# A hybrid mLSTM and DeltaNet block: queries turned from PSUM, mLSTM heads at one step of the units, their outputs written by GpSimd and read further ahead

## The chip, the cores and the metric

One core of a Trainium2 chip runs the whole kernel. The metric is the device time of one execution in microseconds; several runs are made of a kernel and their median is compared. TensorE (PE), VectorE (DVE), ScalarE (ACT), GpSimd (POOL) and SyncE (SP) each work through a queue of their own, in order; DMA transfers are started by SyncE, ScalarE or GpSimd and are carried out beside all of them.

## What is computed

One decoder layer with two branches on 512 tokens of width 2048. The input is normalised and multiplied with one wide matrix w_in; its columns are the inputs of an mLSTM branch (8 heads), of a gated DeltaNet branch (16 heads) and of two merge gates. The part that matters here is the mLSTM head and what becomes of its output:

```python
q = q * (dk ** -0.5)
scores = jnp.einsum('cbhtd,cbhsd->cbhts', qc, kc)
...
num = (inter_w[..., None] * jnp.einsum('bhtd,bhde->bhte', q_c, C)
       + jnp.einsum('bhts,bhse->bhte', intra_w, v_c))
...
h_a = _merge_heads(_rmsnorm(h_a)) * ml_norm_w.astype(jnp.float32)
h_a = h_a * jax.nn.sigmoid(ml_o) * jax.nn.silu(ml_z)
...
y_a = jnp.matmul(h_a, w_out[:ML_WIDTH])
y_b = jnp.matmul(h_b, w_out[ML_WIDTH:])
return jax.nn.sigmoid(gate_a) * y_a + jax.nn.sigmoid(gate_b) * y_b
```

The queries carry the factor 1/sqrt(128); it may as well be put on the keys, since queries and keys only meet in products. The sum with the residual is normalised once more at the end.

## The kernel before

All big products are made of three passes: each operand is split into a high part (`split_hi`, L139, a cast on ScalarE: `wh`) and the rest (`split_lo`, L142, a subtraction on VectorE: `wl`), so a block of weights must be loaded by SyncE, cast and subtracted before TensorE can use it. Weights are loaded four tiles and split three tiles ahead.

The program has four stages.

1. The input is normalised, turned and split, and the first four mLSTM heads' queries and keys are projected (`proj_cm`).
2. `seven_stage` makes the other columns that don't need a convolution, in blocks of two times 512 columns with seven products instead of eight (z, s, q, v and g of the list `SEVEN`). Its sums of weights (`ts`, tag `tg`, three buffers in the pool `wp`) are written to DRAM and read back for the second half of a block. At the end of a block a sink takes the finished tiles out of PSUM: `sink_q` (L730) takes queries and keys of heads 4 to 7. The tiles m1 and m5 come first, U1 and C22, which hold sums in SBUF, after them. Each is scaled or copied on ScalarE, transposed in blocks of 32 by 32 on VectorE into a tile `to` of tag `tg` (L738) and written to DRAM by four DMAs on ScalarE's queue (L744), one of them at each tick, in the arrangement that the heads read later (`qt_d`). Keys are also written unturned (`k_d`, L735).
3. The mixers: eight units (`dn_unit`), each with three projections K, V and Q of two DeltaNet heads. `proj_cm` calls `tick()` 16 times, so a unit has 48 ticks; `tick()` lets generators started with `start(gen, wait)` go on, each up to its next `yield n`, which lets n ticks pass. In this way the order of TensorE's queue is written out by hand: small products of the mixers stand between the big ones. In a unit `dn_front_k` (products `pk`, L902, whose input `kq` is finished by `silu_end`, L837, on VectorE), `dn_front_q`, `dn_back` (products p1 to p4) and `dn_chain` follow each other, partly within the next unit. `ml_head(h)` is started at tick 1 + 42 h. 42 and 46 ticks after its start it multiplies its two output tiles by their gates (`mg`, L1228) and calls `turn(g, hm_d, True)`: a transpose on VectorE into a tile `to` (tag `to`, two buffers, which the values' and the DeltaNet outputs' turns use too, L853), and five ticks later four DMAs of 64 KB into `hm_d` from ScalarE's queue (L863). In the last unit `load_h` (L1248) reads the pairs of `hm_d` back, two pairs ahead, into tiles that the heads have used, and splits each (`uh` on ScalarE, L1245, `ul` on VectorE, L1246).
4. The output projection: two wide blocks with the mLSTM half, one with the DeltaNet half, then blocks with seven products again, and `last_block` for the last 512 columns, for which `load_hm` (L1514) reads tiles of `hm_d` once more, two of them by SyncE and the rest by ScalarE after each split.

TensorE's queue has the order of the code. On the other engines a scheduler orders the instructions, by its own estimate of time and by priority: `urgent(n)` raises it, and `behind("A")` puts an instruction after the newest weight split of that engine ("S": after the newest weight load of SyncE).

Of the kernel before, what the change touches and what calls it, by code (L numbers as in the profile page):

```python
# [15 lines left out]
P = 128  # L16
# [30 lines left out]
UNITS = list(range(8))  # L47
QKS = 2 * QKFIRST * P
# [9 lines left out]
def hybrid_body(  # L58
# [671 lines left out]
    def sink_q(c1, c2, m1, m5, m7, last):  # L730

        def turned(x_, c, a):
            if a:
                with behind("A"):
                    nc.scalar.dma_start(k_d[c], x_)  # L735
            o = spare(True)
            with behind("V"):
                V.transpose(o, x_)  # L738
            to = qt_d[a * 4:(a + 1) * 4].rearrange("h (j r) (n a c) -> r (h j) n a c", r=BS, n=NC, c=BS)
            ov = o.rearrange("p (m c) -> p m c", c=BS)  # L740
            for b in range(4):
                yield 1
                with behind("A"):
                    nc.scalar.dma_start(to[:, :, c, b, :], ov[b * BS:(b + 1) * BS])  # L744

        def out_(ps, t, a, wait):
            z = spare(False)
            with urgent(3):
                A.mul(z, ps, (float(P) ** -0.5, 1.0)[a])
            start(turned(z, t, a), wait + 6 * t)  # L750

        def end5(t):
            add(m5[t], U1[t], m5[t])
            out_(m5[t], t, 1, 8)

        def late_q(t):
            with behind("A"):
                A.mul(U1[t], U1[t], float(P) ** -0.5)
            yield from turned(U1[t], 2 + t, 0)

        def end7(t):
            add(U1[t], U1[t], m7[t])
            start(turned(C22[t], 2 + t, 1), 14 + 6 * t)
            start(late_q(t), 17 + 6 * t)

        return (lambda t: out_(m1[t], t, 0, 4)), end5, end7
# [82 lines left out]
    def turn(src, dst, out=False, lag=5):  # L849


        o = dst if dst is not src and len(dst.shape) == 3 else wk.tile([P, NC, P], F32, tag="to", name="to", bufs=2)
        V.transpose(o if len(src.shape) == 3 else o.rearrange("p n c -> p (n c)"), src)  # L853
        start(travel(o, dst, out, lag > 3), lag if out else 2)

    def travel(o, dst, out, apart):
# [3 lines left out]
        if out:  # L860
            for a in range(4):
                with behind("A"):
                    nc.scalar.dma_start(d[:, :, a, :].rearrange("m r c -> r m c"), ov[a * BS:(a + 1) * BS])  # L863
                if apart:
                    yield 1
            return
# [175 lines left out]
    def dn_chain(j, hs, kq, u, soon):  # L1042
# [60 lines left out]
        turn(g, h_d[h], True, 5 if h < 2 * UNITS[-1] else 3)  # L1103
# [34 lines left out]
    def ml_head(h):  # L1138
# [87 lines left out]
        for i in range(2):  # L1226
            with behind("V"):
                V.tensor_tensor(out=g[i], in0=v1[:, :, i * P:(i + 1) * P], in1=g[i], op=ALU.mult)  # L1228
            turn(g[i], hm_d[2 * h + i], True)
# [18 lines left out]
    def load_h():  # L1248
# [3 lines left out]
        def load():  # L1252
            if len(raws_) < KH:
                if len(raws_) % 2:
                    r = wkb.tile([P, NC, NB + 1], F32, tag="mv1", name="hr", bufs=1)
                    r = r.rearrange("p c n -> p (c n)")[:, 0:2 * S].rearrange("p (a s) -> p a s", s=S)
                else:
                    r = wkb.tile([P, 2, S], F32, tag="mkq", name="hr", bufs=1)
                for n in range(2):
                    load_tile(r[:, n, :], hm_d[2 * len(raws_) + n])  # L1260
                raws_.append(r)

        load()
        load()
        yield 4
        for i in range(KH):
            for n in range(2):
                k = 2 * i + n
                split_scaled(uh[:, k, :], ul[:, k, :], raws_[i][:, n, :], normc[:, 16 + k:17 + k])
# [4 lines left out]
    for h in range(MLH):  # L1274
        start(ml_head(h), 1 + 42 * h, "B")
# [238 lines left out]
    def load_hm():  # L1514
# [3 lines left out]
        def load(q):  # L1518
            r = fin["pool"].tile([P, NO], F32, tag="hmr", name="hmr", bufs=3)
# [4 lines left out]
        for _ in range(2):  # L1524
            load(nc.sync)
        yield 4
# [11 lines left out]
    def sink_last(c1, c2, m1, m5, m7):  # L1538
# [3 lines left out]
        def half_b():  # L1542
# [5 lines left out]
            start(load_hm(), 5)  # L1548
# [185 lines left out]
```

## Time and profile before

| | |
|---|---|
| median of 3 runs | 2212.88 us (2210.53 to 2216.82) |
| profiled execution | 2213.26 us, span 2211.5 us |
| granted TensorE clock, mean | 0.993 |
| ACT's writes hm_d<-to | 64 of 64 KB, 4.1 us to landing |
| ACT's writes qt_d<-to | 32 of 64 KB, 4.0 us to landing |
| SP's reads hr<-hm_d | 16 of 256 KB, 4.2 us to landing |
| hmr<-hm_d | 14 by ACT (4.9 us to landing), 2 by SP (5.4 us) |

In the profile's rows a group or a waiting instruction is named by its line, its operation and its tiles ("kq<-th,kq": kq written from th and kq). A number in square brackets is the time for which the engine stood idle before the instruction, with what released it. A wait for several things is put down to the one that came last.

### The profile page before, as it was taken

The page shows a single profiled execution, that of the slowest core. Times are in us where ns is not written, and L with a number is a line of the kernel's source. Part 1 is how long each engine was busy: PE and PEld are TensorE (multiplying, and loading weights), DVE is VectorE, ACT ScalarE, POOL GpSimd, SP SyncE. Part 2 cuts the span into 40 slices and gives each one's busy share as a digit, 9 for nine tenths or more (in the row PEclk, how much of TensorE's full clock was granted, in tenths as well). Part 3 has the DMA queues.
Part 4 walks back from the last instruction along what each step waited for, and adds up shares of the span by engine and source line. Part 5 has one row for each costly group of instructions (what it writes and reads, how often), then busy time and mean ns, then how long its engine had stood idle before and what let it go on. Part 6 is the DMA issues. An engine that isn't in the chain of part 4 may idle for free.

```text
span 2211.5 us, 31646 instructions
## 1 busy us (share of the span) xinstructions
PE 2146.4 (97%) x10544; PEld 1761.4 (80%) x10544; DVE 1698.6 (77%) x2937; ACT 1035.6 (47%) x1996; POOL 291.4 (13%) x395
## 2 busy tenths in 40 slices
PE   6999999999999999999999999999999999999997
PEld 5877777878887888888888888887877887877785
DVE  5787788788878777777857788778778776578886
ACT  5444444444444444444445545545445464344345
POOL 0320000000000000000012422324314121110200
PEclk9999999999999999999999999999999999999998
DMA  5456676667668757776867677768768577687886
GB/s 157 122 180 189 196 215 191 213 195 231 201 217 240 232 186 231 233 223 189 262 203 176 168 186 183 180 153 208 175 160 213 141 189 193 186 261 212 242 281 222
DMA packets 532006, 444.20 MB, mean 201 GB/s; under 512 B 250369, under 2 KB 385762, under 8 KB 531714
## 3 DMA queue, kind: packets, MB, share of 16 engines
q1 hardware_dynamic: 400946, 350.33, 55.2%
q10 hardware_dynamic: 124192, 74.02, 10.9%
q0 software_dynamic: 6704, 17.83, 3.6%
q8 instruction: 82, 1.34, 0.3%
q14 instruction: 82, 0.67, 0.1%
HBM read 348.66 MB, written 97.58 MB: 202 GB/s over the span
## 4 chain that ended last, share of the span: by engine, by line
PE 65%; DMA 14%; DVE 10%; issue 4%; ACT 2%; SPq 2%; POOL 1%; ACTq 0%; DVEq 0%; POOLq 0%
PE ps L577 11%; PE ps L578 11%; PE ps L576 10%; PE pj L256 8%; PE pj L257 8%; PE pj L258 8%; DVE wl L142 4%; DMA wr<-t_d 3%; DMA wr<-in_w_in_dram 2%; ACT wh L139 2%; DMA wr<-in_w_out_dram 1%; SPq L504 1%; DVE t L518 1%; DMA hr<-h_d 1%; PE py L1369 1%
## 5 line engine op out<-in xcount | busy, mean ns | idle before, releaser
L139 ACT CAST wh<-wr 128x512 fp32r<-128x512 f32 (+1 forms) x522 | 373.1, 717 | 388.8 <-PE pj L257 189.9
L142 DVE TENSOR_TENSOR wl<-wr,wh 128x512 fp32r<-128x512 f32 (+1 forms) x522 | 442.3, 850 | 144.1 <-ACT wh L139 137.1
L256 PE MATMUL pj<-uh,wh 128*128 128x512 f32 x896 | 373.6, 417 | 1.8 <-ACT yp L821 1.8
L258 PE MATMUL pj<-uh,wl 128*128 128x512 f32 x896 | 351.3, 392 | 0.0
L257 PE MATMUL pj<-ul,wh 128*128 128x512 f32 x896 | 350.9, 392 | 0.0
L577 PE MATMUL ps<-wl,uh 128*128 128x512 f32 x752 | 296.8, 395 | 5.7 <-DVE wl L142 5.1
L576 PE MATMUL ps<-wh,uh 128*128 128x512 f32 x752 | 294.7, 392 | 2.7 <-DVE X L630 2.4
L578 PE MATMUL ps<-wh,ul 128*128 128x512 f32 x752 | 294.0, 391 | 0.0
L139 ACT CAST wh<-ts 128x512 fp32r<-128x512 f32 x240 | 148.2, 617 | 256.4 <-DVE ts L536 209.6
L139 ACT CAST wh<-t 128x1024 fp32r<-128x1024 f32 x120 | 126.3, 1052 | 270.1 <-PE ps L578 144.1
L577 PE MATMUL ps<-wl,suh 128*128 128x512 f32 x624 | 243.1, 390 | 4.1 <-DVE wl L142 4.1
L576 PE MATMUL ps<-wh,suh 128*128 128x512 f32 x624 | 243.5, 390 | 1.0 <-ACT wh L139 0.5
L578 PE MATMUL ps<-wh,sul 128*128 128x512 f32 x624 | 242.9, 389 | 0.0
L258 PEld LDWEIGHTS pj<-uh,wl 128*128 128x128 f32 x896 | 168.7, 188 | 37.2
L256 PEld LDWEIGHTS pj<-uh,wh 128*128 128x128 f32 x896 | 169.5, 189 | 32.3 <-ACT yp L821 2.3
L257 PEld LDWEIGHTS pj<-ul,wh 128*128 128x128 f32 x896 | 169.6, 189 | 28.2
L142 DVE TENSOR_TENSOR wl<-ts,wh 128x512 fp32r<-128x512 f32 x240 | 164.4, 688 | 35.2 <-ACT wh L139 35.2
L142 DVE TENSOR_TENSOR wl<-t,wh 128x1024 fp32r<-128x1024 f32 x120 | 147.4, 1228 | 52.6 <-ACT wh L139 51.9
L577 PEld LDWEIGHTS ps<-wl,uh 128*128 128x128 f32 x752 | 141.8, 189 | 44.2 <-DVE wl L142 15.7
L576 PEld LDWEIGHTS ps<-wh,uh 128*128 128x128 f32 x752 | 141.7, 188 | 36.1 <-DVE X L630 6.3
L578 PEld LDWEIGHTS ps<-wh,ul 128*128 128x128 f32 x752 | 141.9, 189 | 28.7
L536 DVE TENSOR_TENSOR ts<-wr 128x512 f32<-128x512 f32 x120 | 82.8, 690 | 100.1 <-DMA wr<-t_d 77.8
(319 smaller groups left out, 3587.6 us busy)
## 6 DMA issues: line engine op xcount, KB each, us to landing
wr<-in_w_in_dram SPq DMA_DIRECT2D x744, 256.0 KB, 3.7
wr<-in_w_out_dram SPq DMA_DIRECT2D x138, 256.0 KB, 4.7
t_d<-ts ACTq DMA_DIRECT2D x104, 256.0 KB, 4.0
wr<-t_d SPq DMA_DIRECT2D x104, 256.0 KB, 3.9
xt<-in_x_dram SPq DMA_DIRECT2D x8, 512.0 KB, 7.4
tg_d<-X ACTq DMA_DIRECT2D x16, 256.0 KB, 5.6
tg_d<-to ACTq DMA_DIRECT2D x16, 256.0 KB, 6.0
v<-v_d SPq DMA_DIRECT2D x8, 512.0 KB, 5.2
```

The lines of the kernel that those rows point to most:

```text
L139: newest["A"] = A.copy(hi, src).ins
L142: newest["V"] = V.tensor_tensor(out=lo, in0=src, in1=hi.bitcast(F32), op=ALU.subtract).ins
L256: T.matmul(ps[j], hi[:, k, wsl], uh[:, kt, :], start=(kt == 0), stop=False)
L257: T.matmul(ps[j], hi[:, k, wsl], ul[:, kt, :], start=False, stop=False)
L258: T.matmul(ps[j], lo[:, k, wsl], uh[:, kt, :], start=False, stop=(kt == KT - 1))
L504: newest["S"] = nc.sync.dma_start(to, src).ins
L518: V.tensor_tensor(out=t13, in0=r[:, 1:3, :], in1=r[:, 0:2, :], op=ALU.subtract)
L536: V.tensor_tensor(out=ts[:, 0, :], in0=r[:, 0, :], in1=r[:, 2, :], op=ALU.subtract)
L576: T.matmul(ps[t], ah, hi, start=(g == "A" and i == 0), stop=False, skip_group_check=True)
L577: T.matmul(ps[t], ah, lo, start=False, stop=False, skip_group_check=True)
L578: T.matmul(ps[t], al, hi, start=False, stop=(i == KH - 1), skip_group_check=True)
L1369: T.matmul(ps[c], uh[:, kt, tsl], hi, start=(kt == ks[0]), stop=False)
```

## The change

Five things are changed together.

- `sink_q`: m1 is transposed straight from PSUM, unscaled; the factor 1/sqrt(128) goes onto the keys (m5 when it is copied, C22 later). The turned tiles come from tag `wr` (`spare(False)`, four buffers of the pool `wp`) and not `tg`. Their four DMAs are issued by GpSimd, two at a tick. k_d is still written by ScalarE.
- `HEADS`: the heads start at 1, 41, 85, 130, 178, 226, 274 and 322 instead of 1 + 42 h; from head 3 on the step is 48, a unit's ticks.
- `turn(..., out)` takes an engine: the mLSTM outputs are written to hm_d by GpSimd, DeltaNet's h_d by ScalarE as before.
- `load_h` keeps three pairs in flight, and puts its splits behind the weights'.
- `load_hm` reads four tiles ahead, behind the weight loads, into two tags in turn, and starts two ticks earlier.

```diff
+HEADS = (1, 41, 85, 130, 178, 226, 274, 322)
...
     def sink_q(c1, c2, m1, m5, m7, last):
 
-        def turned(x_, c, a):
+        def place(o, c, a):
+            to = qt_d[a * 4:(a + 1) * 4].rearrange("h (j r) (n a c) -> r (h j) n a c", r=BS, n=NC, c=BS)
+            ov = o.rearrange("p (m c) -> p m c", c=BS)
+            for b in range(4):
+                G.dma_start(to[:, :, c, b, :], ov[b * BS:(b + 1) * BS])
+                if b % 2:
+                    yield 1
+
+        def turned(x_, c, a, scale):
+            if scale:
+                with behind("A"):
+                    A.mul(x_, x_, float(P) ** -0.5)
             if a:
                 with behind("A"):
                     nc.scalar.dma_start(k_d[c], x_)
-            o = spare(True)
+            o = spare(False)
             with behind("V"):
                 V.transpose(o, x_)
...
-            for b in range(4):
-                yield 1
-                with behind("A"):
-                    nc.scalar.dma_start(to[:, :, c, b, :], ov[b * BS:(b + 1) * BS])
-
-        def out_(ps, t, a, wait):
+            yield 1
+            yield from place(o, c, a)
+
+        def end1(t):
+            o = spare(False)
+            with urgent(3):
+                V.transpose(o, m1[t])
+            start(place(o, t, 0), 2 + 3 * t)
+
+        def end5(t):
+            add(m5[t], U1[t], m5[t])
             z = spare(False)
             with urgent(3):
-                A.mul(z, ps, (float(P) ** -0.5, 1.0)[a])
-            start(turned(z, t, a), wait + 6 * t)
...
+                A.mul(z, m5[t], float(P) ** -0.5)
+            start(turned(z, t, 1, False), 10 + 4 * t)
 
         def end7(t):
             add(U1[t], U1[t], m7[t])
-            start(turned(C22[t], 2 + t, 1), 14 + 6 * t)
-            start(late_q(t), 17 + 6 * t)
+            start(turned(U1[t], 2 + t, 0, False), 16 + 3 * t)
+            start(turned(C22[t], 2 + t, 1, True), 22 + 4 * t)
...
-                with behind("A"):
-                    nc.scalar.dma_start(d[:, :, a, :].rearrange("m r c -> r m c"), ov[a * BS:(a + 1) * BS])
+                with behind("A") if out is nc.scalar else ExitStack():
+                    out.dma_start(d[:, :, a, :].rearrange("m r c -> r m c"), ov[a * BS:(a + 1) * BS])
...
-            turn(g[i], hm_d[2 * h + i], True)
+            turn(g[i], hm_d[2 * h + i], G)
...
-                if len(raws_) % 2:
+                m = len(raws_) % 3
+                if m == 2:
                     r = wkb.tile([P, NC, NB + 1], F32, tag="mv1", name="hr", bufs=1)
...
+                elif m:
+                    r = [wkb.tile([P, NC, P], F32, tag=t, name="hr", bufs=1).rearrange("p c n -> p (c n)") for t in ("mkw", "mw")]
...
-        load()
-        load()
-        yield 4
+        for _ in range(3):
+            load()
+            yield 1
+        yield 1
         for i in range(KH):
             for n in range(2):
                 k = 2 * i + n
-                split_scaled(uh[:, k, :], ul[:, k, :], raws_[i][:, n, :], normc[:, 16 + k:17 + k])
+                with behind("A"), behind("V"):
+                    split_scaled(uh[:, k, :], ul[:, k, :], raws_[i][n], normc[:, 16 + k:17 + k])
...
     for h in range(MLH):
-        start(ml_head(h), 1 + 42 * h, "B")
+        start(ml_head(h), HEADS[h], "B")
...
-            r = fin["pool"].tile([P, NO], F32, tag="hmr", name="hmr", bufs=3)
+            if len(raws_) % 2:
+                r = late["sb"].tile([P, NO], F32, tag="hs", name="hmr", bufs=4)
+            else:
+                r = fin["pool"].tile([P, NO], F32, tag="hmr", name="hmr", bufs=3)
...
-        for _ in range(2):
-            load(nc.sync)
-        yield 4
+        for _ in range(4):
+            with behind("S"):
+                load(nc.sync)
+            yield 1
...
-            start(load_hm(), 5)
+            start(load_hm(), 3)
```

Line numbers of the changed kernel lie one to seventeen above those of before (its `wl` is L143, its casts `wh` L140). What the scheduler makes of it is shown at three places.

ScalarE while the block of queries is turned, before (`wh` are the weight casts, `t` and `ts` the weight sums, `to` the turned tiles):

```order
L744 DMA qt_d<-to 32x16x32 x5
L139 CAST wh<-t_5931 128x1024
L744 DMA qt_d<-to 32x16x32
L139 CAST wh<-ts 128x512
L532 DMA t_d<-ts 128x512
L139 CAST wh<-wr_5843 128x512
L744 DMA qt_d<-to 32x16x32 x2
L735 DMA k_d<-to 128x512
L139 CAST wh<-t_5983 128x1024
```

And in the changed kernel, at the same weight sums:

```order
L140 CAST wh<-t_5928 128x1024
L747 DMA k_d<-to 128x512
L140 CAST wh<-ts 128x512
L533 DMA t_d<-ts 128x512
L140 CAST wh<-wr_5845 128x512
L140 CAST wh<-t_5980 128x1024
L140 CAST wh<-ts 128x512
```

The writes of turned tiles are gone from ScalarE's queue; on GpSimd's they stand as one run of 32. The weight casts, the write of the sums (t_d) and k_d stay.

VectorE in unit 5 about the first product of `dn_front_k`, before (`mg` is a head's output, `kq` the keys that `pk` needs, `aq` made from `pk`, `ke` the turned keys, `tn` a turned solution of the small systems):

```order
L1228 TENSOR_TENSOR mg<-v_14522,mg 128x512
L830 SCALAR_TENSOR_TENSOR kq_14846<-yp_9799,convc,kq_14846 128x512
L837 SCALAR_TENSOR_TENSOR kq_14845<-th,kq_14845 128x512
L853 STREAM_TRANSPOSE to<-mg 128x512
L142 TENSOR_TENSOR wl<-wr,wh 128x512
L964 STREAM_TRANSPOSE tn<-tt 128x256
L830 SCALAR_TENSOR_TENSOR kq_14846<-yp_9799,convc,kq_14846 128x512
L853 STREAM_TRANSPOSE ke<-kq_14845 128x512
L1228 TENSOR_TENSOR mg<-v_14522,mg 128x512
L142 TENSOR_TENSOR wl<-wr,wh 128x512
L985 TENSOR_SCALAR qe<-qe 128x8
L853 STREAM_TRANSPOSE to<-mg 128x512
```

In the changed kernel, in the same unit:

```order
L843 SCALAR_TENSOR_TENSOR kq_14815<-th,kq_14815 128x512
L859 STREAM_TRANSPOSE ke<-kq_14815 128x512
L910 TENSOR_TENSOR aq<-pk,dm 128x4x128
L913 SCALAR_TENSOR_TENSOR jd,nk<-aq,ident 128x128 x3
L143 TENSOR_TENSOR wl<-wr,wh 128x512
L1017 TENSOR_TENSOR vt<-vt,nk 128x512 x2
L913 SCALAR_TENSOR_TENSOR jd,nk<-aq,ident 128x128
L910 TENSOR_TENSOR aq<-pk,dm 128x4x128
L143 TENSOR_TENSOR wl<-wr,wh 128x512
L913 SCALAR_TENSOR_TENSOR jd,nk<-aq,ident 128x128
L1234 TENSOR_TENSOR mg<-v_14830,mg 128x512
```

Before, both outputs and their turns stand among the last steps of kq; now the second kq and both aq stand ahead of the first output.

ScalarE in the last unit, where `load_h` splits what it has read (`uh<-hr`), before (`w` are the copies of `dn_chain`):

```order
L1245 ACTIVATE uh<-hr,normc 128x512
L1067 COPY w<-pw 128x128 x2
L139 CAST wh<-wr 128x512
L836 ACTIVATE th<-vt 128x512
L1245 ACTIVATE uh<-hr,normc 128x512 x3
L139 CAST wh<-wr 128x512
L1245 ACTIVATE uh<-hr,normc 128x512 x2
L139 CAST wh<-wr 128x512
L1067 COPY w<-pw 128x128 x2
```

In the changed kernel:

```order
L1251 ACTIVATE uh<-hr,normc 128x512
L1073 COPY w<-pw 128x128 x2
L140 CAST wh<-wr 128x512
L842 ACTIVATE th<-vt 128x512
L1251 ACTIVATE uh<-hr,normc 128x512
L140 CAST wh<-wr 128x512
L1251 ACTIVATE uh<-hr,normc 128x512
L140 CAST wh<-wr 128x512
L1251 ACTIVATE uh<-hr,normc 128x512
L1073 COPY w<-pw 128x128 x2
```

Before, five splits stand between two pairs of copies, three and two of them in a row; now there are three, each behind a weight cast.

19 lines of the change are left out of this document (6 added, 13 removed).

## The prediction

> **What bounds the kernel now.** I read the page's busy times first, then who waits for whom on TensorE, then that view again in short stretches, to place each wait.
>
> ```profile
> span 2211.5 us, 31646 instructions
> PE 2146.4 (97%) x10544; PEld 1761.4 (80%) x10544; DVE 1698.6 (77%) x2937; ACT 1035.6 (47%) x1996; POOL 291.4 (13%) x395
> ```
> ```profile
> PE pprm L107 <- POOL rs L303: 14.8, 1, 14.8
> PE ps L577 <- DVE wl L142: 9.7, 12, 2.4
> PE pk L902 <- DVE kq L837: 8.6, 4, 5.4
> PE ps L576 <- DVE X L630: 2.4, 3, 0.9
> ```
>
> TensorE is busy for 2146.4 of 2211.5 us, and the change takes no matmul away. So a gain can only come out of the 65.1 us (2211.5 - 2146.4) in which it is idle, and 14.8 of those are the start, which the change doesn't touch. The rest are single waits. These stretches hold the ones near the changed places: 699 to 705 us, 1505 to 1520, 1595 to 1612, 1680 to 1704, 1815 to 1840 and 2165 to 2187, in this order (columns: us in total, times, longest).
>
> ```profile
> PE ps L577 <- DVE wl L142: 2.4, 1, 2.4
> PE ps L576 <- ACT wh L139: 0.2, 1, 0.2
> ...
> PE pk L902 <- DVE kq L837: 1.8, 2, 1.5
> ...
> PE pk L902 <- DVE kq L837: 5.4, 1, 5.4
> ...
> PE pj L256 <- ACT yp L821: 1.8, 1, 1.8
> PE pk L902 <- DVE kq L837: 1.4, 1, 1.4
> ...
> PE pw L1064 <- DVE r L1059: 1.4, 1, 1.4
> PE pr L1056 <- DVE st L1077: 1.4, 1, 1.4
> PE pst L1071 <- ACT w L1067: 1.2, 2, 1.0
> ...
> PE py L1369 <- ACT uh L1245: 1.5, 1, 1.5
> PE py L1369 <- ACT wh L139: 1.1, 1, 1.1
> PE py L1371 <- DVE ul L1246: 1.0, 2, 0.7
> PE py L1370 <- DVE wl L142: 0.4, 1, 0.4
> ```
>
> A long wait costs more than itself: the granted clock falls to half behind it. Three stretches at 0.50 (second number after the busy time) follow the waits at 701, 1605 and 2183 us.
>
> ```profile
> 704.75:708.16 3.41, 3.41 (x10) 0.50 0.80 176
> 1609.28:1616.10 6.83, 5.27 (x17) 0.50 1.09 285
> 2186.13:2189.54 3.41, 3.41 (x9) 0.50 0.00 0
> ```
>
> At half the clock, half of the busy time is lost: 1.7, 2.6 and 1.7 us. So the change can reach, at most: A (the block of queries, 699 to 708) 2.4 + 0.2 + 1.7 = 4.3 us; B (units 4 to 6 of the mixers) 1.8 + 5.4 + 1.8 + 1.4 + 2.6 = 13.0; C (the last unit) 4.0; D (the last block) 4.0 + 1.7 = 5.7. Together 27.0 us. I sum against the profiled execution's own time, 2213.3 us (its span and 1.8 us around it), 0.4 above the median of the runs, 2212.9.
>
> **A: the queries turned from PSUM.** Before, 32 writes to qt_d stand in ScalarE's queue, and the turned tiles share three buffers with the weight sums.
>
> ```profile
> L744 ACTq DMA_DIRECT2D qt_d<-to x32: 309/458/1631, 672.7 to 714.1; - x32
> ...
> 685.49 1.05 ACT L139 CAST wh<-t 128x1024 fp32r<-128x1024 f32 x1 [4.54 <-DMA qt_d<-to]
> 697.02 1.05 ACT L139 CAST wh<-t 128x1024 fp32r<-128x1024 f32 x1 [4.09 <-DMA qt_d<-to]
> ...
> 702.29 0.71 DVE L738 STREAM_TRANSPOSE to<-X 128x512 f32<-128x512 f32 x1 [1.10 <-DMA qt_d<-to]
> ```
>
> ScalarE's next weight cast stands 4.54 and 4.09 us behind such writes, VectorE 1.10 us behind a buffer, and the wait of 2.4 us on wl follows. The change takes all 32 out of that queue (its order in the section on the change shows it) and gives the tiles the four buffers of tag wr. So both releasers go. What it adds: two transposes of 0.71 us at the block's end, urgent on VectorE, where it has its sums to do; two scalings on ScalarE go, with no price, since that engine is 47% busy. The nearest wait for such work at a block's end is 2.4 us over three times, 0.9 at most: bounds 0 and 0.9 us, and I take 0.9, because VectorE is nearly full there. A gives -3.4.
>
> GpSimd has nothing else in that stretch. It has to issue 32 writes of 512 runs of 128 B each, which no row shows. Bounds:
>
> ```profile
> L863 ACTq DMA_DIRECT2D hm_d<-to x64: 309/318/1182, 1208.7 to 1770.1; - x64
> DMA to landing us min/median/max: 2.0/4.0/6.2
> ...
> L811 POOL DMA_DIRECT2D gb<-rows_d x16: 536/618/627, 1150.4 to 1768.3; - x16
> DMA to landing us min/median/max: 4.0/5.0/7.2
> ...
> L1565 POOL DMA_DIRECT2D ty<-tg_d x1: 727/727/727, 2109.1 to 2109.1; - x1
> ```
>
> ScalarE issues the same shape in 0.32 us. GpSimd takes 0.62 us for 128 rows and 0.73 for 256 rows, 0.11 us more. If that step holds, 512 rows cost 0.73 + 2 x 0.11 = 0.95 us; if the cost is in proportion to the rows, 4 x 0.62 = 2.5. I take 1.0, by the pair of rows on GpSimd itself, and keep 0.6 and 2.5 as ends. At 1.0, 32 writes fill 32 of the 41 us in which they were issued before; a tile is due again only after four others, so up to some 2 us each VectorE doesn't meet a buffer still held.
>
> The Trainium skill (DMA: Bandwidth & Descriptors, section "Issuing engines are not separate DMA queues") speaks against this: moving the start of a DMA to another engine saves only the sequencer's time for issuing it, usually small. By it A would be worth nothing and the forecast 3.4 us higher. The rows above speak for A: ScalarE is held not by its issues of 0.46 us, but by what those wait for (4.54 us).
>
> **B: the heads at one step of the units.** A projection has 16 ticks, a unit 48. By the code, dn_front_k's first product pk stands at tick 24 and 25 of a unit, and its input kq is finished (L837) from tick 20 and 23. A head's outputs (mg, L1228, and their transposes) come 42 and 46 ticks after its start. Before, with a step of 42, they fall to ticks 43/47, 37/41, 31/35, 25/29, 19/23, 13/17, 7/11 and 1/5 of units 0 to 7. The waits on pk are in units 4, 5 and 6 alone, where they come ahead of pk. In unit 5 VectorE does this:
>
> ```profile
> 1599.40 0.68 DVE L1228 TENSOR_TENSOR mg<-v,mg 128x512 f32<-128x512 f32 x1
> 1600.67 0.68 DVE L837 SCALAR_TENSOR_TENSOR kq<-th,kq 128x512 f32<-128x512 f32 x1
> ...
> 1604.88 0.69 DVE L1228 TENSOR_TENSOR mg<-v,mg 128x512 f32<-128x512 f32 x1
> ...
> 1610.01 0.68 DVE L837 SCALAR_TENSOR_TENSOR kq<-th,kq 128x512 f32<-128x512 f32 x1
> ```
>
> Both outputs precede the second kq, for which TensorE stood 5.4 us. While they fall to ticks 25 to 41 (units 1 to 3), there is no wait at all:
>
> ```profile
> 1150.00:1450.00 300.00, 300.00 (x1747) 250.94 (x1745) 234.05 (x580) 161.93 (x420) 97.82 (x135) 1.00 0.75 181
> ```
>
> TensorE is busy for 300.00 of 300.00 us there. The new starts put heads 1 to 7 at 35/39, 31/35 and five times 28/32, between positions that cost nothing. All of a head's earlier steps move by the same amount, so they too lie between those of heads 2 and 3 before. For heads 4 to 7 VectorE's order has both kq and the first aq ahead of mg. The wait on yp (1.8 us) belongs to head 6's late position as well. What is late next is the previous unit's dn_back, ticks 25 to 33, beside the four moved operations of 0.7 us. Bounds: nothing, or every one of the 13.0 us back; I leave two waits of 1.4 us, the size of the smaller ones here. B gives 2.8 - 13.0 = -10.2.
>
> With 64 writes of hm_d GpSimd gets 64 x 1.0 = 64 us of work within some 620. Its next work there (nk, dm, ke, we, mkq) is due most of a unit later. ScalarE loses 64 x 0.32 = 20 us of issues, and the waits behind them.
>
> **C and D: reading ahead.** Before, splits of the heads' outputs hold ScalarE until their rows land, in the last unit and in the last block:
>
> ```profile
> 1827.49 1.55 ACT L1245 ACTIVATE uh<-hr,normc 128x512 fp32r<-128x512 f32 x2 [3.83 <-DMA hr<-hm_d]
> ...
> 2168.78 0.72 ACT L1245 ACTIVATE uh<-hmr,normc 128x512 fp32r<-128x512 f32 x1 [4.56 <-DMA hmr<-hm_d]
> ```
>
> The copies w and the weight casts queue behind them, and TensorE waits for those. With three pairs in flight instead of two, a read starts 10 ticks ahead of its split, not 6; in the last block four tiles ahead, not two. How long a tick is, the row of pk tells:
>
> ```profile
> L902 PE MATMUL pk<-kq x128: 270/275/552, 1172.9 to 1790.3; 128*128 128x128 f32 x128
> ```
>
> From unit 0's first to unit 7's last are 617.4 us for 7 x 48 + 1 ticks, 1.83 us each. Four ticks are 7.3 us, more than the 3.83 us; splits now also follow the newest weight split. Against it: head 7 starts 27 ticks later (322, not 295), so its whole work lies in the last unit. The last pair's writes are out by tick 376 and its read comes at 392, so it isn't late. Bounds for C: -4.0 and, if that head's output work costs what head 5's did, +1.4; I leave one wait of 1.4: -2.6. In D the reads share the queues with 8 further reads and weights; half the waits may stay, 2.0: -3.7. Ends 0 and -5.7.
>
> Sum: 3.4 + 10.2 + 2.6 + 3.7 = 19.9 less; 2213.3 - 19.9 = 2193.4, and 2193 for the median.
>
> **The rivals.**
>
> Waits displaced, 24%: the outputs at ticks 28/32 meet dn_back's short products, and each of seven units pays a wait of 1.4 us. That gives 2193 + 7 x 1.4 = 2203; with the clock falling twice, 2206. For it: VectorE has 234 us busy in the 300 quoted. Against it: heads 2 and 3 stood on both sides of this place at no cost.
>
> Depth doesn't help, 13%: SyncE's queue is in order, so an earlier read still stands behind what is queued ahead of it, and C and D stay: 2193 + 2.6 + 3.7 = 2199.
>
> GpSimd's writes become the bound, 9%, and slower: turned outputs of heads and of values share two buffers ("to"). An output's four writes start 5 ticks after its transpose, the two tiles of values come at ticks 36 and 39, and VectorE stands in order behind a buffer not yet landed. Head 2 before had its last write out at tick 43, so its buffer came free 4.0 us later, at 45; nothing waited. Now the eight writes start at tick 33: with 5.0 us to land (2.7 ticks) they meet tick 45 if issued in 9.5 ticks or 17.4 us, that is 2.2 us each. From there on it costs: at 3 us each (24 us) the buffer is 6 us late, seven times, with a half-clock stretch (1.7 us) each: 7 x 7.7 = 54, so 2247. The Trainium skill (SBUF — State Buffer, section "SBUF: two separate sides") has such a mechanism: GpSimd can't write descriptors while VectorE holds their shared port. Against it: 16 issues beside a busy VectorE took 0.54 to 0.63 us.
>
> **How the numbers follow.** The forecast has 52%, and 2% are left for none of these. Low end: all 27.0 us go, 2186, less the 2.3 us by which the fastest run lay under the median: 2184. High end: the displaced waits with the clock, 2206, and A's gain lost as well (3.4), 2210. About 0.3%, or 6.6 us, is what a measurement of this kernel can tell from no change, so faster means under 2206.2. That is the forecast, the rival of depth, and half of the displaced waits: 0.52 + 0.13 + 0.12 = 0.77, less a little for worse in each, 0.75. Slower is GpSimd's rival and a little more, 0.10; the rest, 0.15, is within.
>
> **What would show it.** Right: no wait on wl between 699 and 705 us, GpSimd's writes of qt_d at about 1.0 us, no wait on pk in units 4 to 6, granted clock 1.0 at those places, no hr or hmr ahead of uh on ScalarE. Wrong: writes on GpSimd over 2.2 us with VectorE's transposes of vt waiting for hm_d; TensorE waiting on p, s or tb in every unit; or head 7's work late in the last unit.

## The result and the profile after

The changed kernel takes 2189.84 us (median of 6 runs, 2183.77 to 2193.31), the kernel before 2213.31 us (6 runs, 2210.53 to 2223.08): the ratio is 0.9885, with a 95% interval of 0.9863 to 0.9907. That is 23.5 us less by the medians and 25.5 by the means, which is what the ratio says; 19.9 were forecast. The profiled execution after took 2183.77 us and is the fastest of its six.

The page of the changed kernel, its first lines:

```profile
span 2182.0 us, 31683 instructions
PE 2135.8 (98%) x10544; PEld 1756.6 (81%) x10544; DVE 1709.7 (78%) x2937; ACT 1036.1 (47%) x1994; POOL 349.2 (16%) x491
```

TensorE is idle for 46.2 us instead of 65.1, and its busy time is 10.6 us shorter for the same 10544 matmuls. Part of that is the clock: ahead of the last stretch at the end there were five half-clock stretches (four of 3.41 us, one of 6.83), and now there is one, at 134.6 us, where nothing was changed. The waits on TensorE after (us in total, times, longest):

```profile
PE pprm L108 <- POOL rs L304: 14.6, 1, 14.6
PE ps L578 <- DVE wl L143: 8.3, 14, 1.7
PE put L313 <- DVE xt L290: 2.1, 2, 1.3
PE ps L577 <- DVE X L1406: 1.8, 2, 1.1
PE py L1383 <- DVE wl L143: 1.5, 3, 0.7
```

No row names pk, yp, r, st, w, uh or ul any more. The places A to D are read best from stretches of the trace. Before, each stretch runs from one product of TensorE to a later one (A, C, the 44 us behind C, and D; columns: us, TensorE busy and its matmuls, weight loads, DVE, ACT, POOL, granted clock, share of the DMA engines, GB/s):

```profile
664.10:716.00 51.90, 49.30 (x209) 40.02 (x208) 44.12 (x57) 21.86 (x32) 0.00 (x0) 0.97 0.89 239
1790.00:1845.10 55.10, 51.15 (x319) 41.52 (x318) 43.63 (x106) 31.32 (x62) 6.30 (x6) 1.00 0.65 173
1845.10:1889.10 44.00, 42.64 (x265) 34.75 (x264) 26.80 (x70) 16.08 (x53) 13.29 (x15) 0.96 0.78 192
2150.00:2200.10 50.10, 46.13 (x190) 35.83 (x189) 37.02 (x59) 25.49 (x55) 1.51 (x2) 0.97 0.61 214
```

After, between the same products:

```profile
661.08:708.23 47.15, 47.15 (x210) 39.03 (x208) 43.42 (x56) 20.54 (x30) 20.18 (x32) 1.00 0.84 253
1771.61:1821.70 50.09, 50.09 (x318) 41.82 (x317) 46.29 (x121) 25.78 (x52) 11.51 (x13) 1.00 0.71 186
1821.70:1862.51 40.81, 40.81 (x265) 33.73 (x264) 27.35 (x56) 20.32 (x60) 13.87 (x15) 1.00 0.91 228
2126.21:2168.82 42.61, 42.61 (x189) 35.28 (x188) 33.66 (x54) 24.56 (x53) 0.77 (x2) 1.00 0.67 233
```

TensorE is busy for the whole of each stretch at full clock; A is 4.8 us shorter, C 5.0, the stretch behind it 3.2, D 7.5. For B one row is enough, that of pk:

```profile
L908 PE MATMUL pk<-kq x128: 271/275/377, 1169.0 to 1771.9; 128*128 128x128 f32 x128
```

From the first pk to the last there are 602.9 us, where there were 617.4: 14.5 less. In unit 5 VectorE now works in this order (start, us, operation):

```profile
1588.87 0.68 DVE L843 SCALAR_TENSOR_TENSOR kq<-th,kq 128x512 f32<-128x512 f32 x1
...
1593.46 0.68 DVE L843 SCALAR_TENSOR_TENSOR kq<-th,kq 128x512 f32<-128x512 f32 x1
...
1601.33 0.69 DVE L1234 TENSOR_TENSOR mg<-v,mg 128x512 f32<-128x512 f32 x1
...
1608.64 1.52 DVE L1234 TENSOR_TENSOR mg<-v,mg 128x512 f32<-128x512 f32 x1
```

Both kq are finished 4.6 us apart, where they were 9.3 apart, and the outputs come behind them. GpSimd's writes, by source line (duration in ns, least, median and greatest; first and last start; time to landing of the queries' writes):

```profile
L869 POOL DMA_DIRECT2D hm_d<-to x64: 651/651/757, 1203.0 to 1786.9; - x64
```
```profile
L737 POOL DMA_DIRECT2D qt_d<-to x32: 648/651/833, 666.8 to 708.2; - x32
...
DMA to landing us min/median/max: 2.2/4.7/6.3
```

A write of 512 runs costs GpSimd 0.65 us, not 1.0.

### The profile page after: what moved, and what is told of

It reads as the page before. It is cut to its first block, busy times and chain, and to the rows that moved or that the text cites. A ratio compares the mean times of both kernels' runs of the same rounds, so it can differ in the third digit from the quotient of the medians.

```text
span 2182.0 us, 31683 instructions
## 1 busy us (share of the span) xinstructions
PE 2135.8 (98%) x10544; PEld 1756.6 (81%) x10544; DVE 1709.7 (78%) x2937; ACT 1036.1 (47%) x1994; POOL 349.2 (16%) x491
## 4 chain that ended last, share of the span: by engine, by line
PE 77%; DMA 10%; DVE 6%; issue 3%; ACT 1%; SPq 1%; POOL 0%; ACTq 0%; DVEq 0%; POOLq 0%
PE ps L578 13%; PE ps L579 13%; PE ps L577 12%; PE pj L257 9%; PE pj L259 9%; PE pj L258 9%; DVE wl L143 3%; DMA wr<-t_d 3%; DMA wr<-in_w_out_dram 2%; DMA wr<-in_w_in_dram 2%; PE py L1382 1%; PE py L1384 1%; PE py L1383 1%; ACT wh L140 1%; DMA wr<-t2o_d 1%
## 5 line engine op out<-in xcount | busy, mean ns | idle before, releaser
L140 ACT CAST wh<-wr 128x512 fp32r<-128x512 f32 (+1 forms) x522 | 373.5, 716 | 408.3 <-PE pj L258 229.4
L143 DVE TENSOR_TENSOR wl<-wr,wh 128x512 fp32r<-128x512 f32 (+1 forms) x522 | 434.2, 835 | 112.3 <-ACT wh L140 104.4
L140 ACT CAST wh<-ts 128x512 fp32r<-128x512 f32 x240 | 148.0, 617 | 248.3 <-DVE ts L537 194.1
L140 ACT CAST wh<-t 128x1024 fp32r<-128x1024 f32 x120 | 126.3, 1053 | 268.8 <-PE ps L579 144.5
L143 DVE TENSOR_TENSOR wl<-ts,wh 128x512 fp32r<-128x512 f32 x240 | 164.1, 687 | 35.2 <-ACT wh L140 35.2
L143 DVE TENSOR_TENSOR wl<-t,wh 128x1024 fp32r<-128x1024 f32 x120 | 146.8, 1223 | 51.4 <-ACT wh L140 50.6
```

The costliest lines, as they stand in the source:

```text
L140: newest["A"] = A.copy(hi, src).ins
L143: newest["V"] = V.tensor_tensor(out=lo, in0=src, in1=hi.bitcast(F32), op=ALU.subtract).ins
```

## The same product in two traces

ps, pk and py each follow one another on TensorE in the same order in all these kernels. So the start of the n-th of them in one trace less its start in the trace of before tells how far the kernel is ahead there, and the change of that number over a stretch tells what the stretch gained. This reads single microseconds where two medians can't. The table gives it for the stretches (named by the time in the trace of before), for the changed kernel and for the twelve kernels of the next section (one profile each; negative is faster). "To 1790" is the stretch from the end of B to 1790 us, and so with the others:

| kernel | 125–664 | A 664–716 | 716–1173 | units 0–2 to 1425 | B 1425–1704 | to 1790 | C 1790–1845 | to 1889 | to 2150 | D 2150–2200 | whole span |
|---|---|---|---|---|---|---|---|---|---|---|---|
| changed | -2.9 | -4.8 | +3.9 | 0.0 | -15.4 | +1.0 | -5.0 | -3.2 | +2.8 | -7.5 | -29.5 |
| queries alone | -0.4 | -4.7 | +6.7 | -0.2 | -1.4 | +0.6 | -1.1 | -1.6 | +0.1 | -0.6 | -2.2 |
| starts alone | +0.4 | +0.9 | +7.0 | +0.6 | -15.2 | +1.3 | +0.6 | -2.4 | +0.2 | 0.0 | -6.3 |
| GpSimd alone | +0.2 | +0.7 | +4.6 | +1.1 | -5.3 | 0.0 | -0.8 | -0.1 | +1.0 | -0.8 | +0.6 |
| reads alone | +5.0 | +1.8 | +5.8 | -0.2 | -2.4 | +0.9 | -5.0 | -3.2 | +1.1 | -6.2 | -0.6 |
| all on ScalarE | +0.6 | -4.8 | +4.6 | +0.2 | -14.9 | +1.0 | -5.0 | -3.2 | +1.0 | -7.5 | -27.3 |
| tiles in tg | -0.6 | -4.8 | +6.2 | -0.1 | -15.4 | +1.0 | -5.0 | -3.2 | +1.6 | -7.5 | -27.8 |
| ticks 13/17 | -0.5 | -4.8 | +5.3 | +1.2 | -4.6 | +3.5 | -3.5 | -3.2 | +4.2 | -7.5 | -9.6 |
| starts 42 h | +1.8 | -4.8 | +6.9 | +0.8 | -5.6 | 0.0 | -5.0 | -3.2 | +4.4 | -7.5 | -13.0 |
| writes x4 | -0.1 | -4.8 | +7.0 | +5.2 | -13.4 | +1.7 | -3.7 | -2.9 | +3.3 | -6.4 | -12.4 |
| memsets | -1.2 | -4.8 | +3.7 | +2.3 | -15.4 | +1.0 | -4.8 | -3.2 | +4.2 | -7.4 | -23.2 |
| two pairs | -0.5 | -4.8 | +1.8 | +0.1 | -15.4 | +1.0 | +0.1 | -1.8 | +4.2 | -7.3 | -22.4 |
| two tiles | +0.1 | -4.8 | +2.5 | +0.1 | -15.4 | +1.0 | -4.7 | -3.2 | +4.6 | -0.1 | -20.4 |

Three things come out of it.

The gains sit at A to D, and in the kernels that have the part they repeat to some tenths of a microsecond, since TensorE doesn't wait there at all. But every row is taken against the one profile of before, and what a place cost in that profile is in part chance. Rows of kernels without the part that acts at a place read +0.7 to +1.8 at A, -1.4 and -2.4 at B, -1.1 to +0.6 at C, -0.1, -1.6 and -2.4 behind C, and -0.8 to 0.0 at D. A gain is known no better than that.

With the new starts some eight matmuls of the heads leave B (1642 in it before, 1634 after) for the next stretch. So about 1 us of B's 15.4 comes back as the +1.0 beside it.

The places sum to 35.9 us, and the span fell by 29.5. The other 6.4 are the sum of what lies outside: -0.1 ahead of 125 us, -2.9, +3.9, +1.0, +2.8, and +1.8 behind the last stretch. From 716 to 1173 us nothing was changed, and all thirteen profiles take 1.8 to 7.0 us longer there than the one of before, the three included whose code in that stage is that of before: the profiled execution of before was quick there, by chance. From 1889 to 2150 us the nine kernels with the whole change or most of it are 1.0 to 4.6 us longer, the four with one part 0.1 to 1.1. Some of that may be a price of the change; no run tries it.

## The experiments

Ratios are to the kernel before, run on the same chip, with 95% intervals.

**The queries alone.** `sink_q` of the change in the kernel before; nothing else.

```diff
+                G.dma_start(to[:, :, c, b, :], ov[b * BS:(b + 1) * BS])
...
-            o = spare(True)
+            o = spare(False)
...
+                V.transpose(o, m1[t])
```

> The kernel before with the change of sink_q alone. Theory (each part takes away the waits at its own place): the wait of 2.4 us on wl at 701 us and the half-clock stretch behind it go and nothing else, 3.4 to 4.3 us less than before, a ratio of about 0.998. Rival (moving the start of a write to GpSimd saves only issue time, and ScalarE is not short of time): no change, ratio 1.000, and the wait stays or comes back at another instruction of the same stretch.

Measured: 2214.59 us, ratio 0.9987 (0.9973 to 1.0001). The wait at 701 us and its half-clock stretch are gone, and A is 4.7 us shorter. The timed gain of some 3 us fits, but its interval reaches no change; the stretch carries the verdict.

**The starts alone.** `HEADS` in the kernel before; ScalarE writes hm_d.

```diff
-        start(ml_head(h), 1 + 42 * h, "B")
+        start(ml_head(h), HEADS[h], "B")
```

> The kernel before with the new starts of the heads alone; their outputs are still written by ScalarE. Theory (it is VectorE's order, both kq and both aq ahead of the first mg, that takes away the waits on pk): no wait on pk in units 4 to 6, 10 to 13 us less, ratio 0.994 to 0.995; the waits on hr in the last unit stay. Rival (it is ScalarE's freed queue that cures the units): the waits on pk stay, wholly or for the greater part, 0 to 4 us less, ratio 0.998 to 1.000. Second rival (the waits move to dn_back): the waits on pk go, others of 1.4 us come on p, s or tb, ratio 0.997 to 1.000.

Measured: 2204.20 us, ratio 0.9942 (0.9924 to 0.9959). TensorE has no listed wait between 1480 and 1725 us, and B is 15.2 us shorter, as in the whole change. No other waits came in the units. The last unit kept its waits (from 1795 to 1885 us):

```profile
PE pst L1072 <- ACT w L1068: 2.4, 3, 1.2
PE pw L1065 <- DVE r L1060: 1.8, 1, 1.8
```

So the later head 7 neither helps nor hurts in C by itself (+0.6 us).

**GpSimd's writes of hm_d alone.** The heads at 1 + 42 h, and VectorE's order of mg and kq as before.

```diff
-            turn(g[i], hm_d[2 * h + i], True)
+            turn(g[i], hm_d[2 * h + i], G)
```

> The kernel before with the outputs hm_d written by GpSimd alone; the heads start at 1 + 42 h as before, and VectorE's order of mg, kq and aq stays. Theory (VectorE's order): the waits on pk in units 4 to 6 stay, 5.4 us in unit 5 among them, 0 to 3 us less (ScalarE's waits behind hm_d writes go), ratio 0.9985 to 1.000. Rival (ScalarE's queue): the waits on pk go, 8 to 13 us less, ratio 0.994 to 0.996. Issues of about 0.65 us each, as in the changed kernel, beside a VectorE as busy as before.

Measured: 2214.58 us, ratio 0.9995 (0.9979 to 1.0010). From 1480 to 1725 us the waits on pk are still there:

```profile
PE pk L902 <- DVE kq L837: 6.0, 4, 3.6
```

They shrank, from 8.6 us, and the waits of 1.8 and 1.4 us in unit 6 are gone: B is 5.3 us shorter. The queries and the reads alone, which don't touch B, are 1.4 and 2.4 us shorter there, so some 3 to 4 us are GpSimd's, the upper end of the theory or a little more. So ScalarE's queue had some part in the waits behind a bad order, but the order made them: with the new starts alone they are gone. The time shows none of it beyond its interval.

**The reads alone.** `load_h` and `load_hm` of the change in the kernel before.

```diff
-                if len(raws_) % 2:
+                m = len(raws_) % 3
...
-        for _ in range(2):
-            load(nc.sync)
+        for _ in range(4):
+            with behind("S"):
+                load(nc.sync)
```

> The kernel before with load_h three pairs and load_hm four tiles ahead alone. Theory (depth of reading): the waits on uh, ul and hr in the last unit and on uh in the last block go, with the half-clock stretch at 2186 us, 6 to 10 us less, ratio 0.9955 to 0.997. Rival (SyncE's queue in order, the reads not sooner): 0 to 2 us less, ratio 0.999 to 1.000, and the wait hr to uh of 3.83 us stays. If the four parts add up, the sum of the four gains is near the 23.5 us (ratio 0.9885) of the whole change.

Measured: 2205.98 us, ratio 0.9957 (0.9941 to 0.9974). C is 5.0 us shorter, the stretch behind it 3.2, D 6.2. The four parts alone give 0.9987, 0.9942, 0.9995 and 0.9957; their product is 0.9881, beside 0.9885 for all of them: within the intervals they add up. In B they don't: the starts alone give 15.2 us there, GpSimd alone 5.3, and all together 15.4.

**All writes back on ScalarE.** The changed kernel, with qt_d and hm_d issued by ScalarE; buffers and starts stay.

```diff
-                G.dma_start(to[:, :, c, b, :], ov[b * BS:(b + 1) * BS])
+                with behind("A"):
+                    nc.scalar.dma_start(to[:, :, c, b, :], ov[b * BS:(b + 1) * BS])
...
-            turn(g[i], hm_d[2 * h + i], G)
+            turn(g[i], hm_d[2 * h + i], nc.scalar)
```

> The changed kernel with all 96 writes (qt_d and hm_d) back on ScalarE's queue; the tiles keep the four buffers of wr and the heads their new starts. Theory (in A it is ScalarE's queue that held the weight casts): at 697 to 705 us casts stand behind qt_d again and a wait on wl of 2 to 3 us comes back with its half-clock stretch, 3 to 4 us more than the changed kernel; in the units VectorE's order keeps the waits on pk away, 0 to 1 us; ratio to before 0.990 to 0.991. Rival (moving an issue saves only issue time, the buffers did it): no wait at 700 us, ratio 0.988 to 0.989 as the changed kernel.

Measured: 2188.37 us, ratio 0.9870 (0.9845 to 0.9894): as fast as the changed kernel. The theory of A fell here. ScalarE is held behind qt_d again:

```profile
685.52 1.05 ACT L140 CAST wh<-t 128x1024 fp32r<-128x1024 f32 x1 [3.03 <-DMA qt_d<-to]
...
712.76 1.05 ACT L140 CAST wh<-wr 128x1024 fp32r<-128x1024 f32 x1 [2.98 <-DMA qt_d<-to]
```

Yet TensorE has no wait between 690 and 712 us, and A is 4.8 us shorter all the same. The weight casts could stand 3 us here.

**The turned tiles back in tg.** The changed kernel, written by GpSimd, with the tiles in the buffers that the sums of weights use.

```diff
-            o = spare(False)
+            o = spare(True)
```

> The changed kernel with the turned queries' and keys' tiles in the three buffers of tg again, which the sums of weights ts use too; their writes stay on GpSimd. With all writes on ScalarE and the tiles in wr, the wait on wl at 701 us had stayed away. Theory now (the shared buffers made that wait, not ScalarE's queue): VectorE's sums ts and turns stand behind t_d and qt_d again, and a wait on wl of 2 to 3 us comes back between 695 and 710 us, with a half-clock stretch: the same product of the block of queries starts 3 to 5 us later than in the changed kernel, ratio to before 0.990 to 0.991. Rival (either of the two is enough alone): no wait there, 0 to 1 us, ratio 0.987 to 0.989.

Measured: 2186.08 us, ratio 0.9879 (0.9864 to 0.9895); A 4.8 us shorter, no wait. This theory fell too. Neither the engine nor the tag is needed by itself. What goes with TensorE's wait is seen on VectorE. In the trace of before, from 660 to 720 us, its transposes into `to` wait for a buffer of tg, held by a write of the weight sums or of a turned tile:

```profile
DVE to L738 <- DMA t_d<-ts: 1.5, 2, 1.3
DVE to L738 <- DMA qt_d<-to: 1.1, 1, 1.1
```

VectorE works in order, so the splits wl stand behind them. In the four profiles with the old `sink_q` these waits are 2.6 us (before), 3.1 (starts alone), 3.6 (GpSimd alone) and 4.6 (reads alone), and TensorE's wait on wl at that place is 2.4, 3.1, 3.0 and 4.0. In the ten with the new one, the two just tried among them, there is neither. So the traces speak for buffers of tg that came free too late, and not for ScalarE's hold on the casts by itself. Why the buffers come free in time in this kernel is open: either each part is enough alone, or a third part of `sink_q` did it (m1 turned without a pass over ScalarE, and other ticks). A kernel with the engine and the tag both undone wasn't run.

**Outputs at ticks 13 and 17.** The changed kernel with other starts.

```diff
-HEADS = (1, 41, 85, 130, 178, 226, 274, 322)
+HEADS = (1, 41, 82, 122, 163, 211, 259, 307)
```

> The changed kernel with the heads' starts at 1, 41, 82, 122, 163, 211, 259 and 307, so that the outputs of heads 4 to 7 fall to ticks 13 and 17 of a unit, as in unit 5 of before, and those of head 3 to 20 and 24. Theory (the tick in the unit decides): in four units of the second half the first mg stand ahead of the second kq, and TensorE stands on pk for 3.6 to 5.4 us in each, with a half-clock stretch behind most: 14 to 27 us more than the changed kernel, 2204 to 2217, ratio to before 0.995 to 1.001. Rival (one step for all heads is what counts, or the engine that writes): no waits on pk, ratio 0.988 to 0.990.

Measured: 2203.68 us, ratio 0.9943 (0.9923 to 0.9962). That is 0.0058 over the changed kernel's ratio, 12.8 us of 2213, just under the theory's low end. From 1425 to 1800 us:

```profile
PE pk L908 <- DVE kq L843: 10.2, 6, 4.0
```

The waits come back in every unit from 3 to 7, with one step for the heads 4 to 7 and GpSimd writing: the tick decides whether there is a wait. It doesn't alone decide how long: at the same ticks they were 2.0 us in unit 4, 4.0 in unit 5, 2.8 in unit 6 and 0.7 in unit 7, where 3.6 to 5.4 were expected.

**The starts at 42 h.** The changed kernel, all else as changed.

```diff
-HEADS = (1, 41, 85, 130, 178, 226, 274, 322)
+HEADS = tuple(1 + 42 * h for h in range(8))
```

> The changed kernel with the heads at 1 + 42 h again; all else as changed. Theory (the parts act each at its own place and add up): the waits on pk in units 4 to 6 come back, 5 us in unit 5 among them, 12 to 15 us more between the products of unit 3 and those of the last unit, ratio to before 0.994 to 0.996; A, the last unit and the last block stay free of waits. Rival (GpSimd's writes, freed buffers and deeper reading take over a part of it): waits on pk of 3 us or less, 0 to 7 us more, ratio 0.988 to 0.992.

Measured: 2199.11 us, ratio 0.9933 (0.9917 to 0.9949). From 1480 to 1725 us:

```profile
PE pk L908 <- DVE kq L843: 6.5, 3, 5.0
```

Unit 5's wait of 5.0 us is back; unit 6's is not. B keeps 5.6 us of its 15.4, about as much as GpSimd alone has (5.3), so undoing the starts costs 9.8 us there, or 8.8 with the next stretch, into which matmuls had moved. It is not the 12 to 15 expected. With the new starts GpSimd's part adds nothing, since all on ScalarE has 14.9.

**Two pairs and two tiles again.** The changed kernel with `load_h`, and then with `load_hm`, as before.

```diff
-        for _ in range(3):
-            load()
-            yield 1
+        load()
+        load()
```
```diff
-        for _ in range(4):
-            with behind("S"):
-                load(nc.sync)
+        for _ in range(2):
+            load(nc.sync)
```

> The changed kernel with load_h as before: two pairs ahead, its splits not behind the weights'. Theory (the last unit): waits on st, r, w or wl come back between 1800 and 1830 us and the one near 1850 to 1880 on wl with its half-clock stretch, 4 to 8 us between the last pk and the output projection; the last block stays free of waits; ratio to before 0.990 to 0.992. Rival (the depth of reading was not what mattered there, the heads' starts or the writes on GpSimd did it): no waits, 0 to 1 us, ratio 0.987 to 0.989.

> The changed kernel with load_hm as before: two tiles ahead. Theory (depth in the last block): the waits on uh, ul and wh from 2160 us of the span on come back, 4.0 us, and the half-clock stretch, 1.7: 3.7 to 5.7 us more than the changed kernel, ratio to before 0.990 to 0.991. Rival (the last block gained from load_h or the heads' starts): no waits there, ratio 0.988 to 0.989. With three pairs still read ahead, the last unit and the start of the output projection stay free of waits in both.

Measured: 2192.80 us, ratio 0.9909 (0.9894 to 0.9923), and 2193.36 us, ratio 0.9902 (0.9877 to 0.9926). With two pairs, from 1795 to 1885 us:

```profile
PE pst L1077 <- ACT w L1073: 1.5, 2, 1.1
PE pr L1062 <- DVE st L1083: 1.1, 1, 1.1
PE py L1376 <- DVE wl L143: 1.1, 1, 1.1
PE pw L1070 <- DVE r L1065: 0.9, 1, 0.9
```

With two tiles, from 2130 to 2178 us:

```profile
PE py L1382 <- ACT wh L140: 2.0, 1, 2.0
PE py L1382 <- ACT uh L1251: 1.3, 1, 1.3
```

Each undoes its own place: C goes from -5.0 to +0.1 and the stretch behind it from -3.2 to -1.8, D from -7.5 to -0.1. The timed runs alone don't tell either kernel from the changed one, as the intervals overlap; the stretches do. Two things stay unparted. `load_h` both reads deeper and puts each split behind a weight split, and only the two together were tried; `load_hm` both reads deeper and starts earlier.

**GpSimd's writes four times over.** Three more to scrap memory behind each write of hm_d.

```diff
+                    for _ in range(3 if out is G else 0):
+                        d2 = dr.tile([16, BS, BS], F32, tag="scrap", name="scrap", bufs=192)
+                        out.dma_start(d2.rearrange("m r c -> r m c"), ov[a * BS:(a + 1) * BS])
```

> The changed kernel with every write of hm_d issued four times by GpSimd, three of them to scrap memory that nobody reads: some 2.6 us for what was 0.65. Theory of the threshold (2.2 us for each write, from the two buffers of to): eight writes fill 20.8 us instead of the 17.4 that are free, VectorE's turns of vt stand up to 3.4 us or more behind hm_d in seven units, and TensorE with them, 24 to 36 us more than the changed kernel, 2214 to 2226, ratio to before 1.000 to 1.006. Rival (VectorE and the values have that much time in hand): waits on hm_d show on VectorE, but little on TensorE, 0 to 6 us more, ratio 0.988 to 0.991.

Measured: 2199.47 us, ratio 0.9920 (0.9896 to 0.9943), 0.0035 over the changed kernel's ratio or 7.7 us: far under the theory and a little over the rival (the two intervals overlap slightly). From 1150 to 1850 us:

```profile
PE pw L1073 <- DVE r L1068: 2.9, 6, 1.1
PE pk L911 <- DVE kq L843: 1.8, 1, 1.8
PE pr L1065 <- DVE st L1084: 0.9, 1, 0.9
```

The writes of one head's two outputs, scrap and all, took 23.1 us (1280.2 to 1303.3), over the 17.4 of the rival, and still VectorE never waited for hm_d or scrap: the next turn of values came at 1303.9 and needed the first output's buffer alone, whose writes had landed at 1296.2. So the threshold of 2.2 us was wrong: it charged that turn with the last write of both outputs. GpSimd itself waited:

```profile
POOL scrap L872 <- DMA scrap<-to: 7.8, 11, 1.3
POOL hm_d L869 <- DMA hm_d<-to: 3.7, 6, 1.2
```

**GpSimd busy without traffic.** Twelve memsets of 128x64 behind each write of hm_d.

```diff
+                        idle = wk.tile([P, BS * 2], F32, tag="idle", name="idle", bufs=1)
+                        for _ in range(12):
+                            G.memset(idle, 0.0)
```

> The changed kernel with twelve memsets of 128x64 on GpSimd behind each write of hm_d: about as much of GpSimd's time as the three scrap writes took (1.95 us), and no traffic. The four-fold writes cost some 9 us in the mixers. If that came of GpSimd's time (its other operations, ke, kq, gz and tb among them, come later): 6 to 12 us more than the changed kernel again, ratio to before 0.991 to 0.994. Rival (it came of 12.6 MB more of traffic and of slower landings): 0 to 2 us more, ratio 0.987 to 0.9895.

Measured: 2188.39 us, ratio 0.9894 (0.9878 to 0.9910), no difference from the changed kernel that can be told. Its row shows that it isn't the test it was meant to be:

```profile
L873 POOL MEMSET idle<- x768: 141/151/186, 1149.9 to 1453.9; 128x64 f32 x192
```

The scheduler ran the memsets ahead, all in the first half of the mixers. There, 116 us more of GpSimd's time (768 x 0.151) cost one wait of 2.2 us; in the second half, nothing was tried. Whether the four-fold writes cost their 7.7 us through GpSimd's time or through traffic stays open.

## Why the prediction was right, and where its steps were not

**The sum** came near (2193 forecast, 2189.84 measured), and the likeliest case came true: no displaced wait in the units, earlier reads helped, GpSimd's writes were no bound. That it came so near is in part luck. All four terms were too small, 19.9 us for 31.8 (or 35.0 with the stretch behind C). Against that stand the 6.4 us by which the changed kernel's profile takes longer outside these places, most of them in stretches that the change doesn't touch, and 6.1 us by which that profile lies under the median of its runs.

**The bound of 27.0 us** was near for the places it listed: the changed kernel takes 4.8, 14.5 (from the first pk to the last), 5.0 and 7.5 us from them, 31.8 us. In the stretches of before, idle time and lost clock give 2.6 + 1.6 for A, 4.0 for C and 4.0 + 1.5 for D (0.03 of 50.1 us). A, C and D gained 0.6 to 2 us more. The trace of before shows most of that for A and D. Where TensorE isn't held, the matmuls of these places start 0.23 us apart but are shown 0.39 us long, so a listed wait begins some 0.16 us late; and one or two of the next starts come 0.34 us apart and not 0.23. Together that is 1.6 of D's 2.0 us, for five waits, and 0.5 of A's 0.6: a listed wait of TensorE costs some 0.3 us more than its row says.

**A, -3.4:** measured -4.8. The wait went, but the step "So both releasers go" took ScalarE's hold on the casts for a cause of its own, and that failed: with all 32 writes back in ScalarE's queue a cast stands 3 us behind them and TensorE doesn't wait. The traces speak for the other releaser, VectorE behind the buffers of tg, in which ScalarE's queue may still have had a part. The wait of 0.9 us left for two urgent transposes did not come. The Trainium skill (DMA: Bandwidth & Descriptors, section "Issuing engines are not separate DMA queues") says that moving the start of a DMA saves only the time to issue it; the experiment agrees, as with the tiles in wr the engine was worth nothing in A. As a rival in the prediction it failed all the same: A was to be worth nothing by it, and was worth 4.8 us by other parts of the change.

**B, -10.2:** measured -14.5. The mechanism, the tick of mg against kq, was right: the starts alone give 15.2 us in B (13.9 with the next stretch), and ticks 13 and 17 bring the waits back. Mis-sized was the remainder: 2.8 us were left for two waits on dn_back; none came.

**C, -2.6:** measured -5.0, and D, **-3.7:** measured -7.5. The changed reads were right and worth all of both places, as the two kernels with the old reads show; how much of C is depth and how much the new place of the splits wasn't parted. The waits kept back (1.4 and 2.0) did not come. One sign of being right came only in part: in the last block ScalarE's splits still wait for hmr, 3.6 us in three times where it was 6.5 before, but no product waits for them. What the prediction lacked is the wait of 1.4 us on wl at 1879 us with its half-clock stretch, behind the last unit: 3.2 us. It was in the trace, not in the stretches that were read. With the new reads it is gone each time, but not all of the 3.2 us is theirs. The three other kernels with the old reads are 0.1 (GpSimd alone), 1.6 (queries) and 2.4 us (starts) shorter there, with waits of 1.2, 1.4 and 0.4 us, and the half-clock stretch came in the first of them alone.

**GpSimd's price, 1.0 us:** measured 0.651, at the lower end. The step "If that step holds, 512 rows cost 0.73 + 2 x 0.11 = 0.95 us" failed: 512 runs cost hardly more than the 0.62 us of 128 rows, and less than the 0.73 of 256. The threshold of 2.2 us also had a slip (12 ticks less 2.7 are 9.3, not 9.5), which changes little. The Trainium skill (SBUF — State Buffer, section "SBUF: two separate sides") has GpSimd locked out of writing descriptors while VectorE runs an operation in a mode that takes the port pair they share. The 64 writes beside a VectorE that is busy 570 of 700 us took 0.651 to 0.757 us, so no run here shows it.

**The base.** The sum was made against the profiled execution, and that of before was some 5 us quicker than the other profiles between 716 and 1173 us, while its total lay at the median; so it was slower than usual elsewhere, B and the stretch behind C among the places (by the rows without the part that acts there). The one of after was 6.1 us under its median.

## What to carry to other kernels

An output that nobody waits for can still stop TensorE when its steps stand, on an in-order engine, ahead of those that feed the next product: write down at which tick each falls in the repeated unit, and look for the ticks at which the trace shows no wait. An engine that is held for 4.5 us is not by itself a cause; undo that part alone, and look for a wait that comes and goes with TensorE's in all the profiles. Where single runs scatter by 10 us, compare the start of the same product in two traces; but take more than one profile of the kernel before, since a place that was slow there by chance shows up as a gain in every row.

## What the runs showed of the hardware

- The same wait of 1.65 us near 132 us of the span was followed by a half-clock stretch near 134 us in eight of the fourteen profiles, in six not; a wait of 1.1 to 1.4 us behind the last unit was, in two profiles of four. Waits of that length lie at the edge, and what they cost in clock is 0 or 1.7 us by chance. Ahead of the last one in each profile, the stretches last 3.41 us or twice that. The Trainium skill (TensorE: Matmul & The Clock Gate, section "HAM oscillation — how this bites in real kernels") warns of idle gaps over about 3.4 us; here half of that was enough at times, so the measurement decides.
- With the writes four times over, GpSimd issued its ninth at 1285.85 us, just behind the landing of the first (1285.56), and waited for a landing 17 times: eight writes in flight, the new one included, was the most seen at any issue. What sets it, the queue or the program's semaphores, was not tried.
- The reads of hmr took longer to land when four were ahead (7.6 us in the median of all 16, 5.4 before), and no product waited for them.
